# The residual of a decoder's first layer: from load, add and store to accumulating stores onto a copy of x in DRAM

## The chip, the cores and the metric

The kernel runs on one core of one Trainium2 chip. The metric is the device time of one execution in microseconds (us). One further execution was taken with the hardware profiler; its rows are what the text quotes. Engines are named as the profile names them: PE does matmuls, PEld its weight loads, DVE, ACT and POOL work on tiles in on-chip memory, SP only issues transfers. A q behind a name (SPq) is that engine's instruction queue.

## What is computed

Two layers of a decoder over 2048 positions of width 1024. The first layer normalises x, multiplies it with one large input projection, runs four heads of forgetting attention and four of stick-breaking attention, multiplies their outputs with a gate, multiplies with an output projection and adds x. The second layer does the like with three groups of dilated windows.

```python
def even_layer(x, g_norm, w_in, b_f, g_q, g_k, w_out):
    h = rmsnorm(x, g_norm)
    proj = h @ w_in
    ...
    mixed = jnp.concatenate([merge_heads(fox), merge_heads(sb)], axis=-1) * jax.nn.silu(gate)
    return x + mixed @ w_out
```

The change is about the last line: the sum `x + mixed @ w_out`, called x1 here, 2048 x 1024 numbers of four bytes, 8.39 MB. The second layer reads x1 twice: at its start, to normalise it, and at its end, for its own residual.

## The kernel before

**Products.** Every large product is split into panels: 1024 rows of the left side (a round, `r`) by 512 columns. `panel_steps` (L261) computes a panel with seven products of half the size, by the recursive scheme that needs seven where the plain one needs eight, and each number is split into a high and a low part, so that a product is three matmuls (`mm3`, L88, its lines 91 to 93). The names A11, A12, S2, S3, S1, A22, S4 are the seven left and right factors. A panel ends in four results, each of two tiles `c` of 128 x 512 in PSUM plus the parts kept before. `result` (L307) makes each `c` with a DVE addition (L300) in a buffer of the tag `res`, of which there are four, and hands it to an emitter.

**Right factors.** `Weights` (L184) loads quarters of the weight matrix into four buffers `wraw` (L216, SP's queue, 512 KB each). POOL forms the sums and differences among them (L226). ACT writes the high part (L81), DVE or POOL the low part (L86), into one of four buffers `wop`, which PE multiplies with. `get` (L251) keeps three of them ready.

**Left factors.** `left` (L342) reads the transposed input back from DRAM in pieces `lp` (L362), forms sums with DVE and POOL (L345) and splits them (L81 and L86).

**The output projection of the first layer** has four panels: two rounds of rows, two halves of columns. Its emitter is `residual` (L947): for each `c` it loads the 256 x 256 block of x that belongs to it into a tile `x1t` (L953), adds on DVE (L954) and stores the sum into x1 (L955). There are 32 such blocks. Both transfers stand in SP's queue. When a round's x1 is stored, `transpose_to` (L153) loads its rows (L157), normalises and transposes them for the second layer.

**Order.** The program text is emitted by Python generators, and a list scheduler then orders the instructions of each engine by its own model of durations, with the data dependencies as bounds. Each engine takes its queue strictly in order, and an instruction that waits for a semaphore holds up all that stands behind it on its engine. Transfers are issued by SP alone in the kernel before; the launch line (L1334) sets `dynamic_dma_scratch_size=512`, the bytes of a partition that are kept for the descriptors of transfers that POOL issues.

Of the kernel before, what the change touches and what calls it, by code (L numbers as in the profile page):

```python
# [12 lines left out]
OP = mybir.AluOpType  # L13
# [4 lines left out]
P = 128  # L18
# [18 lines left out]
class K:  # L37
# [28 lines left out]
    def c2(self, shape=(P, CH), dt=F32, name="c2", tag="c"):  # L66

        return self.cs.tile(list(shape), dt, name=name, tag=tag, bufs={"c": 4, "res": 4}.get(tag, 2))
# [439 lines left out]
def identity(k):  # L508
    jp = k.c2([P, P], name="jp")
    k.nc.gpsimd.iota(jp, pattern=[[1, P]], base=0, channel_multiplier=-1,  # L510
                     allow_small_or_imprecise_dtypes=True)
    k.ident = k.consts.tile([P, P], F32, name="ident")
    k.nc.vector.tensor_scalar(k.ident, jp, 0.0, None, op0=OP.is_equal)
# [47 lines left out]
def each(emit):  # L561

    def run(block, half, cs):
        for g, c in enumerate(cs):
            emit(block, half, g, c)
    return run
# [188 lines left out]
def merged(*gens):  # L755

    live = [[g, n, 0] for g, n in gens]
    while live:
        live.sort(key=lambda e: (e[2] + 0.5) / e[1])
        e = live[0]  # L760
        if next(e[0], "end") == "end":
            live.remove(e)
        e[2] += 1

def even_attention(k, tail):
    tc, nc = k.tc, k.nc
    c2 = k.c2
    scale = float(P) ** -0.5  # L770
# [2 lines left out]
    def load_head(kind, h):  # L773
        T, V = (k.fT, k.v["f"]) if kind == "f" else (k.sT, k.v["s"])
        kt = k.big([P, 4, 2, CH], F32R, name="kt")
        vt = k.big([P, 4, 2, TPC, P], F32R, name="vt")

        def chunk(c):
            s = slice(c * CH, (c + 1) * CH)
            nc.sync.dma_start(kt[:, c].bitcast(F32), T["k"][:, h, :, s].bitcast(F32))  # L780
            for z in range(2):
                nc.sync.dma_start(vt[:, c, z].bitcast(F32),
                                  V[s, z, h * P:(h + 1) * P].rearrange("(j p) d -> p j d", p=P).bitcast(F32))

        heads[kind, h] = kt, vt
        return chunk

    def load_q(kind, h, u):
        T = k.fT if kind == "f" else k.sT
        if kind == "f" and u % 2 == 0:  # L790
            c = u // 2
            bias[h, c] = c2(name="bias")
            nc.sync.dma_start(bias[h, c], k.ncum[h:h + 1, c * CH:(c + 1) * CH].to_broadcast([P, CH]))
        q = c2([P, 2, 2 * P], F32R, name="qT", tag="q")
        nc.sync.dma_start(q.bitcast(F32), T["q"][:, h, :, u * 2 * P:(u + 1) * 2 * P].bitcast(F32))
        return q
# [52 lines left out]
    def pv(kind, h, u, rows):  # L849

        vt = heads[kind, h][1]
        po = k.ps("s" if kind == "f" else "t")
        gt = c2([P, 2 * P], name="gate", tag="pT")
        m = (0 if kind == "f" else 4) + h
        cols = slice(u * 2 * P, (u + 1) * 2 * P)
        nc.sync.dma_start(gt, k.gT[:, m, cols])

        def transposed(jj):
            pt = k.ps("t")
            hl = k.wps.tile([P, 2, 2, 2 * P], F32R, name="pT", tag="wp")  # L860
            for jx in range(2):
                for i in range(jx if jj == u else 0, 2):
                    nc.tensor.transpose(pt[:, (jx * 2 + i) * P:(jx * 2 + i + 1) * P],  # L863
                                        rows[:, i, (jj * 2 + jx) * P:(jj * 2 + jx + 1) * P], k.ident)
            flat = [hl[:, z].rearrange("p j t -> p (j t)") for z in range(2)]
            for s in (slice(0, 2 * P), slice(3 * P, 4 * P)) if jj == u else (slice(0, 4 * P),):
                k.split(flat[0][:, s], flat[1][:, s], pt[:, s])
            return hl

        ready = transposed(0)  # L870
        for jj in range(u + 1):
            yield
            hl = ready
            if jj < u:
                ready = transposed(jj + 1)
            for jx in range(2):
                j = jj * 2 + jx
                i0 = P if jj == u and jx else 0
                a = [vt[:, j // TPC, z, j % TPC] for z in range(2)]
                k.mm3(po[:, i0:2 * P], a, [hl[:, z, jx, i0:] for z in range(2)], j == 0, j == 2 * u + 1)  # L880
        nc.vector.tensor_tensor(gt, po[:, :2 * P], gt, op=OP.mult)
        nc.sync.dma_start(k.mixT[:, m, cols], gt)
# [3 lines left out]
    def slopes(g, hf):  # L886

        t = k.w4([P, HG, 2, P], name="slopes")
        for h in range(HG):
            slope = 2.0 ** (-8.0 * (g * HEADS + hf * HG + h + 1) / (3 * HEADS))  # L890
            nc.gpsimd.tensor_scalar(t[:, h], k.dist, -slope32(slope) * GROUPS[g][1], 1.0, op0=OP.mult, op1=OP.mult)
        nc.sync.dma_start(k.bias[g, hf], t)
# [10 lines left out]
    for n, (kind, h, u) in enumerate(units):  # L903
        rows = k.big([P, 2, S], name="rows")
        rest = k.big([P, 2, S], name="rest") if kind == "s" else None
        gens = [(qk(kind, h, u, q, rows, rest), 2 * (u // 2 + 1))]
        if n + 1 < len(units):
            q = load_q(*units[n + 1])
        if (kind, h, u) == ("f", 0, 0):
            k.table()  # L910
        nxt = order.index((kind, h)) + 1
        if u == 1 and nxt <= 6:
            slopes((nxt - 1) // 2, (nxt - 1) % 2)
        if nxt < len(order) and u >= 3:
            if u == 3:
                chunk = load_head(*order[nxt])
            else:
                chunk(u - 4)
        if len(past) == 2:
            v = past.pop(0)  # L920
            gens.append((pv(*v[0], v[1]), v[0][2] + 1))
        merged(*gens)
        past.append(((kind, h, u), rows))
        if nxt == len(order) and u in (5, 6):

            tail()
# [4 lines left out]
def odd_layer(k, x, x1, even_w_out, w_in, w_out, out):  # L931
    tc, nc = k.tc, k.nc
    c2, dr = k.c2, k.dram
# [13 lines left out]
    def residual(r, n):  # L947
        def emit(block, half, g, src):
            t0 = r * ROUND + block * CH + g * 256
            c0 = n * CH + half * 256  # L950
            view = lambda d: d[t0:t0 + 256, c0:c0 + 256].rearrange("(r p) c -> p r c", p=P)
            a = c2([P, 2, 256], name="x1t")
            nc.sync.dma_start(a, view(x))  # L953
            nc.vector.tensor_tensor(a, src.rearrange("p (r c) -> p r c", r=2), a, op=OP.add)  # L954
            nc.sync.dma_start(view(x1), a)  # L955
        return each(emit)

    def two(A, emits, tick, after=None):
# [337 lines left out]
@with_exitstack  # L1296
def tile_hybrid_trunk(ctx, tc, x, even_norm, even_w_in, even_b_f, even_q_gain, even_k_gain, even_w_out,
                      odd_norm, odd_w_in, odd_q_gain, odd_k_gain, odd_w_out, out):
    k = K(ctx, tc)
    k.table()  # L1300
    x1 = k.dram.tile([S, D], F32, name="x1d")
    A = []
    spare = []
    first = left_direct(k, x[0], even_norm, A, spare)
    next(first)
    identity(k)
    late = lambda: constants(k, k.cs, even_norm, odd_norm, even_b_f, even_q_gain, even_k_gain, odd_q_gain, odd_k_gain)
    even_projection(k, x[0], even_w_in[0], first, A, spare, late)
    odd = odd_layer(k, x[0], x1, even_w_out[0], odd_w_in[0], odd_w_out[0], out[0])
    W, first = next(odd)  # L1310

    def tail():
        W.ahead(1)
        next(first)

    even_attention(k, tail)
    k.table()
    next(odd, None)

# [27 lines left out]
```

## Time and profile before

| | us |
|---|---|
| median of three runs | 2823.75 |
| lowest and highest of them | 2819.15, 2825.49 |
| the profiled execution, its own time | 2826.53 |
| its span in the trace | 2824.8 |
| first L953 to last L955 in that trace | 1281.3 to 1534.4 |

The span is what the trace covers; the time of the same execution is 1.7 us more. A row of a group of instructions gives the line, the engine, the output and input tiles, shapes and count, then the busy time and the mean of one in nanoseconds, then the idle time of the engine just before these instructions and what ended it. In a list of waits, a row is the waiting instruction, the one waited for, the time in total, how often, and the longest. A row of a stretch gives its length and each engine's busy time with the count of instructions, then the granted clock of PE, the busy share of the 16 DMA engines, and GB/s.

### The profile page before, as it was taken

How to read it: one execution, taken by the hardware profiler on the slowest of the kernel's cores; microseconds unless marked ns; L12 is line 12 of the kernel's file. 1: busy time of each engine (PE TensorE's matmuls, PEld its weight loads, DVE VectorE, ACT ScalarE, POOL GpSimd, SP SyncE). 2: the span in 40 equal slices, each digit the busy share in tenths (PEclk: the TensorE clock that was granted, in tenths of full speed). 3: DMA queues.
4: the chain of work that ended last, by engine and by line, in shares of the span. 5: the costliest groups of instructions: out<-in, count | busy, mean ns of one | idle time of the engine just before them, and what ended most of it. 6: DMA issues, size and time to landing. Idle time of an engine off the chain costs nothing.

```text
span 2824.8 us, 55621 instructions
## 1 busy us (share of the span) xinstructions
PE 2676.4 (95%) x20191; PEld 2455.5 (87%) x20191; DVE 2052.7 (73%) x4373; ACT 1618.6 (57%) x3924; POOL 1223.4 (43%) x981
## 2 busy tenths in 40 slices
PE   6999999999999999998987999999989999999998
PEld 5898878998787789987887999999889999999876
DVE  7857684684888888888959857476797686763966
ACT  6465553454776666665364555555664577665642
POOL 3545464544544433326545544343245432422322
PEclk9999999999999999999998999999999999999999
DMA  5576544445433344435577553334543445444675
GB/s 180 181 222 210 172 160 154 154 142 192 144 111 118 112 123 144 139 104 173 187 232 246 154 179 107 121 122 146 169 128 126 139 140 166 132 147 134 219 254 183
DMA packets 398770, 449.43 MB, mean 159 GB/s; under 512 B 31712, under 2 KB 331040, under 8 KB 398496
## 3 DMA queue, kind: packets, MB, share of 16 engines
q1 hardware_dynamic: 398496, 445.89, 49.4%
q8 instruction: 159, 2.61, 0.4%
q14 instruction: 115, 0.94, 0.1%
HBM read 291.22 MB, written 154.57 MB: 158 GB/s over the span
## 4 chain that ended last, share of the span: by engine, by line
PE 62%; DVE 21%; DMA 7%; ACT 5%; issue 3%; POOL 1%; SPq 1%; DVEq 0%; ACTq 0%; POOLq 0%
PE ps L91 17%; PE ps L93 17%; PE ps L92 17%; DVE rest L828 4%; PE ps L863 2%; PE ps L1145 2%; DVE wop L86 2%; DVE A L86 2%; PE ps L1135 2%; PE ps L1116 2%; DVE lp L345 1%; DVE S L86 1%; PE ps L1061 1%; DVE pT L86 1%; DVE c L300 1%
## 5 line engine op out<-in xcount | busy, mean ns | idle before, releaser
L226 POOL TENSOR_TENSOR wraw<-wraw 128x512 f32<-128x512 f32 (+1 forms) x320 | 444.2, 1400 | 430.3 <-DVE wop L86 157.1
L81 ACT ACTIVATE wop<-wraw 128x512 fp32r<-128x512 f32 (+1 forms) x560 | 349.5, 629 | 383.4 <-PE ps L93 294.2
L86 POOL TENSOR_TENSOR wop<-wraw,wop 128x512 fp32r<-128x512 f32 (+1 forms) x240 | 329.4, 1375 | 534.0 <-ACT wop L81 503.8
L92 PE MATMUL ps<-wop,S 128*128 128x256 f32 (+1 forms) x1792 | 512.4, 286 | 18.1 <-DVE wop L86 16.8
L91 PE MATMUL ps<-wop,A 128*128 128x256 f32 (+1 forms) x1792 | 512.0, 287 | 14.2 <-DVE c L300 13.5
L91 PE MATMUL ps<-wop,S 128*128 128x256 f32 (+1 forms) x1792 | 515.8, 289 | 9.9 <-DVE c L300 6.3
L92 PE MATMUL ps<-wop,A 128*128 128x256 f32 (+1 forms) x1792 | 511.7, 286 | 2.2 <-DVE wop L86 1.5
L93 PE MATMUL ps<-wop,S 128*128 128x256 f32 (+1 forms) x1792 | 512.9, 287 | 0.0
L93 PE MATMUL ps<-wop,A 128*128 128x256 f32 (+1 forms) x1792 | 509.5, 285 | 0.0
L86 DVE TENSOR_TENSOR wop<-wraw,wop 128x512 fp32r<-128x512 f32 (+1 forms) x320 | 270.2, 845 | 232.0 <-ACT wop L81 230.6
L92 PEld LDWEIGHTS ps<-wop,S 128*128 128x128 f32 x1792 | 343.3, 192 | 21.0 <-DVE wop L86 17.8
L91 PEld LDWEIGHTS ps<-wop,A 128*128 128x128 f32 x1792 | 342.3, 191 | 19.0 <-issue 13.4
L91 PEld LDWEIGHTS ps<-wop,S 128*128 128x128 f32 x1792 | 342.1, 191 | 15.1 <-issue 8.4
L92 PEld LDWEIGHTS ps<-wop,A 128*128 128x128 f32 x1792 | 342.9, 191 | 4.0 <-DVE wop L86 3.2
L93 PEld LDWEIGHTS ps<-wop,S 128*128 128x128 f32 x1792 | 342.7, 191 | 3.3 <-issue 2.6
L93 PEld LDWEIGHTS ps<-wop,A 128*128 128x128 f32 x1792 | 342.7, 191 | 1.4 <-issue 0.8
L300 DVE TENSOR_TENSOR c<-u,ps 128x512 f32<-128x512 f32 (+1 forms) x274 | 178.7, 659 | 91.9 <-PE ps L93 86.1
L81 ACT ACTIVATE pT<-ps 128x512 fp32r<-128x512 f32 (+2 forms) x352 | 165.5, 504 | 135.6 <-PE ps L863 81.3
L831 POOL TENSOR_TENSOR rows<-rows,rest 128x512 f32<-128x512 f32 (+4 forms) x160 | 152.6, 957 | 162.1 <-DVE rest L828 141.8
L86 DVE TENSOR_TENSOR pT<-ps,pT 128x512 fp32r<-128x512 f32 (+2 forms) x352 | 188.0, 559 | 44.2 <-ACT pT L81 42.8
L1128 ACT ACTIVATE row<-row,nm 128x256 f32<-128x256 f32 (+1 forms) x384 | 172.5, 452 | 64.4 <-DVE nm L1126 63.9
L92 PE MATMUL ps<-pT,vt 128*128 128x256 f32 x576 | 171.1, 299 | 5.5 <-DVE pT L86 5.3
(214 smaller groups left out, 6485.0 us busy)
## 6 DMA issues: line engine op xcount, KB each, us to landing
wraw<-in_odd_w_in_dram SPq DMA_DIRECT2D x88, 512.0 KB, 4.0
wraw<-in_even_w_in_dram SPq DMA_DIRECT2D x70, 512.0 KB, 4.2
ld<-qk SPq DMA_DIRECT2D x106, 256.0 KB, 3.2
qk<-c SPq DMA_DIRECT2D x96, 256.0 KB, 2.4
lp<-hT SPq DMA_DIRECT2D x60, 256.0 KB, 3.6
uu<-ot SPq DMA_DIRECT2D x96, 132.0 KB, 1.9
fin<-uu SPq DMA_DIRECT2D x16, 792.0 KB, 4.5
hT<-te SPq DMA_DIRECT2D x48, 256.0 KB, 4.3
```

The costliest lines, as they stand in the source:

```text
L81: nc.scalar.activation(hi, src, AF.Copy)
L86: (nc.vector if lo_on == "dve" else nc.gpsimd).tensor_tensor(lo, src, hi.bitcast(F32), op=OP.subtract)
L91: mm(out, a[0], b[0], start=start, stop=False, skip_group_check=more)
L92: mm(out, a[0], b[1], start=False, stop=False, skip_group_check=more)
L93: mm(out, a[1], b[0], start=False, stop=stop, skip_group_check=more)
L226: tt = lambda e, o, x, y, op, s: e.tensor_tensor(o[:, s], x[:, s], y[:, s], op=op)
L300: nc.vector.tensor_tensor(out[g], x[g], y[g], op=OP.add)
L828: nc.vector.tensor_tensor_scan(o[:, b:b + n][:, ::-1], back, k.ident[:, :1].to_broadcast([P, n]), 1.0 if carry is None else carry, OP.mult ...
L831: nc.gpsimd.tensor_tensor(dst[:, :w], dst[:, :w], o[:, b + 1:b + 1 + w], op=OP.mult)
L863: nc.tensor.transpose(pt[:, (jx * 2 + i) * P:(jx * 2 + i + 1) * P], rows[:, i, (jj * 2 + jx) * P:(jj * 2 + jx + 1) * P], k.ident)
L1116: nc.tensor.matmul(scores(hp, e), q[pr, za, hp], ring[pr, zb, hp, blocks], start=i == 0, stop=i == 2)
L1128: nc.scalar.activation(row[:, h // 2, h % 2, :nk], row[:, h // 2, h % 2, :nk], AF.Exp, bias=nm[:, h:h + 1], accum_out=ot[:, HW + HG + h:HW ...
```

## The change

DVE's addition and the tile `x1t` go. For each 128 rows x 256 columns of `c`, POOL now issues a transfer that adds onto what stands in x1 (`accum_op=OP.add`): 64 of 128 KB in place of 32 loads and 32 stores of 256 KB. So that x1 holds x by then, SP copies x to x1 in DRAM in 16 transfers of 512 KB. The calls of the copies are put among the units of the first layer's attention, but nothing in their data binds them to that place.

```diff
-def even_attention(k, tail):
+def even_attention(k, tail, residual):
...
         nxt = order.index((kind, h)) + 1
+        if n % 4 == 1:
+            residual(n // 4)
         if u == 1 and nxt <= 6:
...
             view = lambda d: d[t0:t0 + 256, c0:c0 + 256].rearrange("(r p) c -> p r c", p=P)
-            a = c2([P, 2, 256], name="x1t")
-            nc.sync.dma_start(a, view(x))
-            nc.vector.tensor_tensor(a, src.rearrange("p (r c) -> p r c", r=2), a, op=OP.add)
-            nc.sync.dma_start(view(x1), a)
+            for i in range(2):
+                nc.gpsimd.dma_start(view(x1)[:, i], src[:, i * 256:(i + 1) * 256], accum_op=OP.add)
         return each(emit)
...
-    even_attention(k, tail)
+    def residual(i):
+        k.nc.sync.dma_start(x1[i * P:(i + 1) * P], x[0][i * P:(i + 1) * P])
+
+    even_attention(k, tail, residual)
```

The launch line is unchanged and becomes L1337. Where the scheduler puts the new transfers is seen in the order of the instructions. On POOL, in the output projection of the first round of rows (the rows L226, L345 and L86 are the right factors' sums, the left factors' sums and the low parts), there stood before:

```order
L226 TENSOR_TENSOR wraw<-wraw 128x512 x2
L86 TENSOR_TENSOR wop<-wraw,wop 128x2x256
L226 TENSOR_TENSOR wraw<-wraw 128x512 x2
L86 TENSOR_TENSOR wop<-wraw,wop 128x2x256 x3
L345 TENSOR_TENSOR lp<-lp 128x512
L226 TENSOR_TENSOR wraw<-wraw 128x512 x7
```

and now, in the same projection (L955 is the accumulating transfer):

```order
L955 DMA x1d<-c 128x256 x4
L226 TENSOR_TENSOR wraw<-wraw 128x512 x2
L955 DMA x1d<-c 128x256 x4
L226 TENSOR_TENSOR wraw<-wraw 128x512 x2
L955 DMA x1d<-c 128x256 x4
L226 TENSOR_TENSOR wraw<-wraw 128x512 x2
L86 TENSOR_TENSOR wop<-wraw,wop 128x2x256 x2
L226 TENSOR_TENSOR wraw<-wraw 128x512 x2
L86 TENSOR_TENSOR wop<-wraw,wop 128x2x256
L345 TENSOR_TENSOR lp<-lp 128x512
L86 TENSOR_TENSOR wop<-wraw,wop 128x2x256
L955 DMA x1d<-c 128x256 x8
```

The 64 transfers stand in 20 groups of two to eight, between the sums and splits that feed PE; 44 of them directly follow another.

On SP, at the start of the program, behind the load of the last small constant (`ok`), there stood before:

```order
L546 DMA ok<-in_odd_k_gain_dram 128x64
L216 DMA wraw<-in_even_w_in_dram 128x4x256 x3
L673 DMA sqT<-fb 128x512 x3
L216 DMA wraw<-in_even_w_in_dram 128x4x256
L673 DMA sqT<-fb 128x512
```

and now:

```order
L546 DMA ok<-in_odd_k_gain_dram 128x64
L1317 DMA x1d<-in_x_dram 16x8192 x6
L216 DMA wraw<-in_even_w_in_dram 128x4x256
L1317 DMA x1d<-in_x_dram 16x8192 x2
L216 DMA wraw<-in_even_w_in_dram 128x4x256
L1317 DMA x1d<-in_x_dram 16x8192 x8
L216 DMA wraw<-in_even_w_in_dram 128x4x256
L673 DMA sqT<-fb 128x512 x3
```

All 16 copies (L1317) have moved ahead of the whole first layer, among the first weight loads. On DVE, in the same projection as above, there stood before (x1t is the tile of the residual):

```order
L300 TENSOR_TENSOR c_15852<-u3_15671,ps_15794 128x512 [waits DVE_49,PE_49]
L345 TENSOR_TENSOR stage_15650<-stage_15650,lp_16084 128x512 [waits DVE_49]
L954 TENSOR_TENSOR x1t_15856<-c_15852,x1t_15856 128x512 [waits DMAHW2_49,DVE_49]
L300 TENSOR_TENSOR c_15853<-u3_15671,ps_15795 128x512 [waits PE_49]
L86 TENSOR_TENSOR wop_15895<-wraw_15471,wop_15895 128x2x256 [waits Activation_49]
```

The additions that make `c` (L300) now wait for POOL's transfers (DMASW is the semaphore of one of these), because a buffer of `c` is free only when its two transfers have landed:

```order
L300 TENSOR_TENSOR c_15860<-u3_15679,ps_15802 128x512 [waits DMASW0_49,DMASW1_49,DVE_49,PE_49]
L300 TENSOR_TENSOR c_15861<-u3_15679,ps_15803 128x512 [waits DMASW2_49,DMASW3_49,DVE_49,PE_49]
L86 TENSOR_TENSOR wop_15899<-wraw_15483,wop_15899 128x2x256 [waits Activation_49]
L300 TENSOR_TENSOR c_15926<-u3_15679,ps_15868 128x512 [waits DMASW5_49,DMASW4_49,PE_49]
L345 TENSOR_TENSOR lp_16301<-lp_16301,lp_16303 128x512 [waits DMAHW3_49,DMAHW4_49,DMAHW0_49,Pool_49]
L300 TENSOR_TENSOR c_15927<-u3_15679,ps_15869 128x512 [waits DMASW7_49,DMASW6_49,PE_49]
```

L954 is gone there, and the waits for DMASW have come to L300.

## Prediction

> **What bounds the kernel now.** I read the page first, then stretches, then the output projection by itself.
>
> ```profile
> span 2824.8 us, 55621 instructions
> PE 2676.4 (95%) x20191; PEld 2455.5 (87%) x20191; DVE 2052.7 (73%) x4373; ACT 1618.6 (57%) x3924; POOL 1223.4 (43%) x981
> ```
>
> PE is busy for 95% of the span, so time can be won only where PE waits. The view of stretches (busy time and count of PE, PEld, DVE, ACT, POOL, then clock, DMA share, GB/s) shows such a place:
>
> ```profile
> 1320.00:1535.00 215.00, 177.92 (x1394) 174.47 (x1394) 173.14 (x234) 107.10 (x234) 119.72 (x77) 0.92 0.71 232
> 1535.00:1750.00 215.00, 202.12 (x1689) 198.42 (x1687) 155.38 (x303) 116.03 (x297) 119.83 (x87) 0.96 0.48 152
> ```
>
> The first stretch holds 31 of the 32 old additions. PE idles there for 215 - 178 = 37 us, in the equal stretch behind it for 13 us. DVE is the busiest of the others (173 us), POOL has 215 - 120 = 95 us idle, and the DMA engines are at 71%. PE's longest waits in this stretch, and the chain that ended last in it by line, say who is late:
>
> ```profile
> PE ps L92 <- DVE wop L86: 13.7, 6, 8.4
> PE ps L91 <- DVE c L300: 11.5, 2, 10.3
> ...
> by line: issue 13.0%; DVE S L86 9.6%; DVE x1t L954 7.1%; DVE A L86 6.4%; DVE wop L86 5.7%; DMA hT<-te 5.3%; DVE c L300 4.5%; PE ps L91 3.7%; DVE lp L345 3.7%; ACT te L149 3.6%; PE ps L92 3.5%; PE ps L93 3.4%; DMA x1t<-in_x_dram 3.2%; DMA lp
> ```
>
> PE waits for DVE, and DVE's queue holds the additions of the residual.
>
> **What goes.** 32 additions, of which 31 lie in the stretch:
>
> ```profile
> L954 DVE TENSOR_TENSOR x1t<-c,x1t 128x512 f32<-128x512 f32 x31 | 31.2, 1008 | 9.0 <-DMA x1t<-in_x_dram 8.9
> ```
>
> DVE loses 31.2 us of work and 9.0 us of waiting. On the chain it was 7.1% + 3.2% of 215 us = 22 us (the additions, and the loads of x that they waited for). That is the most that the removal can give; what is late next is DVE's splitting of S and A, which stays. SP loses 64 issues at about 0.37 us each, which nobody waited for by themselves. The 8.39 MB of loads of x leave the stretch; an accumulation has to read the same bytes of x1 again, so the DMA engines are not relieved.
>
> **What is added on POOL.** 64 transfers. POOL issues none in the trace of before, so the cost is bounded by the nearest rows: SP's issue of the old store, and its time from issue to landing.
>
> ```profile
> L955 SPq DMA_DIRECT2D x1d<-x1t x32: 359/370/1312, 1320.0 to 1534.4; - x32
> ...
> DMA to landing us min/median/max: 2.1/4.1/8.4
> ...
> mixT<-gate SPq DMA_DIRECT2D x64, 128.0 KB, 2.1
> ```
>
> From below it is 0.37 us, if POOL only hands the transfer over. From above it is the whole time to landing, if POOL cannot write the next one's descriptors until the last one is through. Between the two stands POOL's own kind of work, 1.5 to 1.6 us an instruction:
>
> ```profile
> L226 POOL TENSOR_TENSOR wraw<-wraw 128x512 f32<-128x512 f32 x32 | 47.7, 1514 | 11.1 <-DMA wraw<-in_even_w_out_dram 9.8 <-DVE wop L86 1.3
> L86 POOL TENSOR_TENSOR wop<-wraw,wop 128x512 fp32r<-128x512 f32 x24 | 38.3, 1599 | 42.6 <-ACT wop L81 26.9 <-ACT lg L106 15.7
> ```
>
> I take the upper bound. The reason is in the program: L1337 keeps 512 bytes of a partition for the descriptors of POOL's transfers. A transfer here has 128 rows, each of which is read in two places (`c` and x1) and written in one, over 16 DMA engines; I judge that so small a store holds one such transfer and not two, so that a transfer directly behind another waits until that one has landed. [...] No run so far shows it.
>
> For the landing I take 4.1 us, the median of the old stores of 256 KB, since an accumulation of 128 KB carries as much: 128 KB out of `c` and 128 KB read from x1. Its lower end is 2.1 us, which is also what a plain 128 KB store takes, its upper end 8.4 us. So:
>
> - 44 transfers directly behind another: 44 x 4.1 = 180 us.
> - 20 behind one to fifteen other POOL instructions of some 1.5 us, half of the landing hidden: 20 x 2.05 = 41 us.
> - POOL's own work in the stretch: 119.7 us, of which nothing goes.
>
> The sum is 341 us in a stretch of 215 us: POOL becomes the bound, and +126 us is left over. None of it can hide. Behind the waiting transfers stand L226 and L86, which make the right factors for PE, with three `wop` kept ready, some few us of PE's work; and DVE's L300 waits for the landing of the transfers four tiles back, with DVE's L86 behind it in its queue. POOL still has to wait for ACT and for weights at times; of its 95 us idle I add 10 us. The removed 22 us are then worth nothing, since they were DVE's.
>
> [...]
>
> **What is added at the start.** The 16 copies move 8.39 MB. In the first 25 us the DMA engines moved 274 GB/s at 82% busy:
>
> ```profile
> 0.00:25.00 25.00, 8.78 (x36) 7.47 (x37) 14.63 (x33) 18.03 (x40) 3.33 (x9) 1.00 0.82 274
> 50.00:75.00 25.00, 18.84 (x122) 16.65 (x121) 24.29 (x34) 13.63 (x28) 21.40 (x15) 0.81 0.32 112
> ...
> 23.16 9.60 SPq L216 DMA_DIRECT2D wraw<-in_even_w_in_dram  x3
> 40.30 0.39 SPq L216 DMA_DIRECT2D wraw<-in_even_w_in_dram  x1
> 48.24 0.38 SPq L216 DMA_DIRECT2D wraw<-in_even_w_in_dram  x1
> ...
> 53.11 3.01 POOL L226 TENSOR_TENSOR wraw<-wraw 128x512 f32<-128x512 f32 x2
> ...
> 70.85 0.80 PE L93 MATMUL ps<-A,wop 128*128 128x512 f32 x1 [4.20 <-DVE wop L86]
> ```
>
> At that rate they take 31 us, from 23 us on, and the three weight loads that stood at 23 to 33 us are now interleaved with them, the last behind all 16. The loads at 40 and 48 us follow in the queue, and the first sums that need them begin on POOL at 53.1 us. If all of this slips, the copies cost up to 31 us less the slack; I reckon that the copies end near 23 + 31 = 54 us and the last load comes some 6 us late. DVE, busy for 24.3 of the 25 us, is what PE waits for at 70.85 us, so part of that is covered: +4 us, with 0 and 30 us as ends.
>
> **The sum.** 126 + 10 + 4 = +140 us on the profiled execution's own 2826.5 us (span 2824.8 us and 1.7 us around it) gives 2966 us. The median of the runs lies 2.8 us lower, so I forecast 2963 us, 4.9% slower.
>
> **The rivals.**
>
> *POOL pays for the writing alone* (slower, but little): the store of descriptors holds several transfers, and one costs what POOL's other instructions cost, 1.5 us. 64 x 1.5 = 96 us; with its own 120 us POOL is at 216 of 215 us. For it speaks that POOL sat idle for 95 us; against it that idle time came in pieces before other engines' results (26.9 us before ACT's L81 in the row of L86), so they can't all be filled. I give it +20 us after a few us from DVE: about 2845 us, between 2830 and 2870. Chance 0.14.
>
> *The change does what it is written to do* (faster): a transfer costs POOL 0.37 us as it costs SP, 64 x 0.37 = 24 us, and fits in the 95 us. Then DVE's 22 us on the chain come off, less 4 us at the start: 2824 - 18 = 2806 us. For it speaks that DVE is what PE waits for; it decides as long as a transfer holds POOL for less than about 1 us. Chance 0.10.
>
> *No change*: a transfer holds POOL for about 1 us, and what DVE gains POOL and the start give back: 2818 to 2829 us. Chance 0.04.
>
> My forecast has the remaining 0.72. Its own range has the landing as its largest unknown: at 2.1 us the sum is 92 + 21 + 120 = 233 us, +18 us with 10 for waits, 2852 us; at 6.25 us, halfway between median and longest, 275 + 62 + 120 = 457 us, +242 us and 14 more, 3080 us.
>
> **The range and the chances.** Eight times in ten: 2840 to 3070 us. That leaves out the faster case and no change (0.14) and about 0.06 of the ends. Within 0.2%, or 5.6 us, is about what a measurement of this kernel can't tell from no change: its three runs spread over 6.3 us. Faster by more than that 0.10, within it 0.04, slower 0.14 + 0.72 = 0.86.
>
> **What would show it right or wrong.** Right: in the stretch of the output projection, some 350 us long, POOL has no room, the time between two L955 in a row is near the landing of the first, POOL's rows L226 and L86 stand idle behind L955, and PE's longest waits there are for wop (POOL's or, behind it, DVE's) or for DVE's L300 that waits for a transfer. Wrong: two L955 in a row within 1.5 us of each other while the first is still under way; then the descriptors fit, and one of the rivals holds. Wrong as well if PE's waits at 50 to 75 us grow by tens of us: then the copies are the cost, and not POOL. If the stretch gets shorter than 215 us, DVE's additions were worth what the chain says.

## The result, and the profile after

| | us |
|---|---|
| before, median of four runs beside the changed kernel | 2824.62 |
| after, median of four runs | 2951.48 (2945.13 to 2953.09) |
| ratio, with its 95% interval | 1.0443 (1.0431 to 1.0456) |
| span of the profiled execution, before and after | 2824.8 and 2951.3 |

The change costs 127 us; 140 were forecast. Where they arise is found by following the same instruction through both traces. The last L881, the gates at the end of the first layer's attention, starts at 1312.2 us before and 1318.4 after: +6. The first L1018, behind the output projection, starts at 1547.1 and 1678.4: +131. The last store of the result, L1274, is at 2821.2 and 2947.7: +126.5. So 125 us are lost in the output projection and 6 ahead of it, and about 5 are given back behind it.

The view of stretches of the kernel after (columns as in the prediction) has the projection:

```profile
1324.00:1662.00 338.00, 203.46 (x1412) 197.94 (x1410) 152.99 (x209) 109.99 (x237) 160.54 (x141) 0.77 0.53 128
```

For nearly as many matmuls as before (1412 records, 1394 before) the projection takes 338 us in place of 215. PE idles for 135 us of it, where it idled for 37: of the 123 us by which the stretch has grown, 98 are PE's idle time, and 25 are a longer busy time for the matmuls. DVE is down from 173 to 153 us of work. POOL's share looks modest, 161 of 338 us, because the 138.1 us that it waits ahead of its transfers are not counted as busy. The view of the source line of the transfers shows them:

```profile
L955 POOL DMA_DIRECT2D x1d<-c x64: 862/881/1023, 1324.6 to 1660.8; - x64
...
  issue: 138.1, 44
...
DMA to landing us min/median/max: 3.1/3.1/7.8
```

"issue" is idle time for which the profile sees no other instruction as the cause. It comes 44 times, 138.1 us in all or 3.14 us each. With POOL's 160.5 us of work that is 299 of 338 us. 41 of the 44 stand ahead of a transfer that directly follows another. The other three such transfers wait as well, 8.7 us in all, but there the profile names an instruction of ACT or DVE as the cause; and three waits called "issue" stand ahead of the first transfer of a group. On the chain that ended last in this stretch, "issue" of all engines together is 37.9% of 338 us, or 128 us, where it was 13.0% of 215 us, or 28 us, before. One group in the timeline of POOL (start, duration, and in brackets the idle time ahead and its cause) shows the wait:

```profile
1524.15 0.89 POOL L955 DMA_DIRECT2D x1d<-c  x1 [2.62 <-issue]
1530.31 0.87 POOL L955 DMA_DIRECT2D x1d<-c  x1 [5.26 <-issue]
1533.73 0.88 POOL L955 DMA_DIRECT2D x1d<-c  x1 [2.55 <-issue]
```

In each cycle 0.88 us is POOL's own record of the transfer (its writing, as it is called here; no row shows what POOL does in it), and the rest is waiting. The view of L955 narrowed to one transfer at a time gives the landing of each, counted from its own start. The first of these three lands after 5.8 us, and the second starts 6.16 us behind it; the second lands after 3.1 us, and the third starts 3.42 us behind it. So it is for all 44 transfers that directly follow another: the transfer ahead takes between 3.1 and 6.0 us to land, 3.7 on average, and the next one starts 0.26 to 0.36 us after that landing. The longest waits of PE in the same stretch, ACT's wait for POOL and DVE's for a transfer say who passes it on:

```profile
PE ps L92 <- POOL wop L86: 57.1, 7, 15.5
PE ps L91 <- ACT wop L81: 50.5, 6, 16.8
...
ACT wop L81 <- POOL wraw L226: 89.8, 11, 26.8
...
DVE c L300 <- DMA x1d<-c: 9.9, 2, 5.7
```

Before, PE waited 1.4 us for POOL's L86 there. Now it waits 57 us for it and 50 us for ACT's L81, which in turn waits 90 us for what POOL's L226 has to sum (29.5 us before). L86 and L226 are the instructions that stand in POOL's queue behind the transfers. DVE's own wait for a landing, 9.9 us in two places, is small.

At the start, the copies and the loads beside them keep the DMA engines busy for the whole of a 25 us stretch, and the sums that stood at 53.1 us begin at 62.5 us:

```profile
25.00:50.00 25.00, 23.54 (x114) 19.06 (x114) 21.75 (x34) 13.88 (x29) 5.17 (x4) 1.00 1.00 351
...
62.53 10.40 POOL L226 TENSOR_TENSOR wraw<-wraw 128x512 f32<-128x512 f32 x6 [5.93 <-DMA wraw<-in_even_w_in_dram]
```

Of these 9.4 us three are left at the first L828 (714.7 us before, 717.6 after).

### The profile page after: what moved, and what is told of

Same layout as the page of the kernel before. It is cut to its first block, busy times and chain, and to the rows that moved or that the text cites. A ratio compares the mean times of both kernels' runs of the same rounds, so it can differ in the third digit from the quotient of the medians.

```text
span 2951.3 us, 55618 instructions
## 1 busy us (share of the span) xinstructions
PE 2704.6 (92%) x20191; PEld 2479.0 (84%) x20191; DVE 2025.4 (69%) x4341; ACT 1619.4 (55%) x3924; POOL 1260.5 (43%) x1045
## 3 DMA queue, kind: packets, MB, share of 16 engines
q0 software_dynamic: 9216, 8.39, 2.3%
HBM read 291.22 MB, written 162.96 MB: 154 GB/s over the span
## 4 chain that ended last, share of the span: by engine, by line
PE 60%; DVE 18%; issue 7%; ACT 5%; DMA 4%; POOL 4%; SPq 0%; DVEq 0%; POOLq 0%; ACTq 0%
PE ps L91 16%; PE ps L92 16%; PE ps L93 16%; DVE rest L828 4%; PE ps L863 2%; PE ps L1145 2%; PE ps L1116 2%; PE ps L1135 2%; DVE wop L86 2%; DVE A L86 1%; POOL wraw L226 1%; PE ps L1061 1%; DVE lp L345 1%; DVE pT L86 1%; POOL x1d L955 1%
## 5 line engine op out<-in xcount | busy, mean ns | idle before, releaser
L226 POOL TENSOR_TENSOR wraw<-wraw 128x512 f32<-128x512 f32 (+1 forms) x320 | 445.3, 1414 | 429.7 <-DVE wop L86 156.7
L81 ACT ACTIVATE wop<-wraw 128x512 fp32r<-128x512 f32 (+1 forms) x560 | 349.5, 629 | 460.1 <-PE ps L93 304.5
L91 PE MATMUL ps<-wop,S 128*128 128x256 f32 (+1 forms) x1792 | 520.7, 292 | 65.4 <-ACT wop L81 50.5
L92 PE MATMUL ps<-wop,A 128*128 128x256 f32 (+1 forms) x1792 | 514.7, 287 | 43.2 <-POOL wop L86 43.1
L92 PE MATMUL ps<-wop,S 128*128 128x256 f32 (+1 forms) x1792 | 519.0, 290 | 25.8 <-POOL wop L86 18.9
L86 POOL TENSOR_TENSOR wop<-wraw,wop 128x512 fp32r<-128x512 f32 (+1 forms) x240 | 325.0, 1367 | 492.9 <-ACT wop L81 479.6
L93 PE MATMUL ps<-wop,S 128*128 128x256 f32 (+1 forms) x1792 | 517.6, 289 | 0.0
L86 DVE TENSOR_TENSOR wop<-wraw,wop 128x512 fp32r<-128x512 f32 (+1 forms) x320 | 272.8, 854 | 271.0 <-ACT wop L81 267.9
L91 PEld LDWEIGHTS ps<-wop,S 128*128 128x128 f32 x1792 | 346.6, 194 | 72.3 <-ACT wop L81 54.2
L92 PEld LDWEIGHTS ps<-wop,A 128*128 128x128 f32 x1792 | 345.2, 193 | 45.3 <-POOL wop L86 44.1
L92 PEld LDWEIGHTS ps<-wop,S 128*128 128x128 f32 x1792 | 348.7, 195 | 29.7 <-POOL wop L86 19.5
L93 PEld LDWEIGHTS ps<-wop,S 128*128 128x128 f32 x1792 | 348.6, 195 | 3.2 <-issue 2.6
L300 DVE TENSOR_TENSOR c<-u,ps 128x512 f32<-128x512 f32 (+1 forms) x274 | 178.9, 659 | 146.4 <-PE ps L93 129.7
L81 ACT ACTIVATE pT<-ps 128x512 fp32r<-128x512 f32 (+2 forms) x352 | 165.4, 502 | 138.7 <-PE ps L863 83.2
L86 DVE TENSOR_TENSOR pT<-ps,pT 128x512 fp32r<-128x512 f32 (+2 forms) x352 | 188.0, 559 | 45.4 <-ACT pT L81 43.8
L300 DVE TENSOR_TENSOR u<-u,ps 128x512 f32<-128x512 f32 (+1 forms) x168 | 109.5, 658 | 104.9 <-PE ps L93 104.3
```

What stands on the lines that cost most here:

```text
L81: nc.scalar.activation(hi, src, AF.Copy)
L86: (nc.vector if lo_on == "dve" else nc.gpsimd).tensor_tensor(lo, src, hi.bitcast(F32), op=OP.subtract)
L91: mm(out, a[0], b[0], start=start, stop=False, skip_group_check=more)
L92: mm(out, a[0], b[1], start=False, stop=False, skip_group_check=more)
L93: mm(out, a[1], b[0], start=False, stop=stop, skip_group_check=more)
L226: tt = lambda e, o, x, y, op, s: e.tensor_tensor(o[:, s], x[:, s], y[:, s], op=op)
```

## Theories and experiments

The theory is that of the prediction: the store of descriptors, 512 bytes, holds one accumulating transfer, and POOL stands still until that one has landed. It is theory A here, beside the expectations' theory B. By it two such transfers fit in 576 bytes and three in 960, and three plain ones, or three of 64 rows, in 512; these counts were the author's estimate, and no run had shown them. The main rivals: the writing itself costs POOL's time; an accumulating transfer is slow work for the DMA engines; the copies are in the way. Ratios are to the kernel before, measured beside each kernel, with 95% intervals. Where two kernels have the same order of instructions on every engine, the text says so; where it doesn't, the scheduler has also moved other instructions.

**The size of the store.** Only the launch line is edited, and the order stays that of the changed kernel.

```diff
-dynamic_dma_scratch_size=512
+dynamic_dma_scratch_size=576
```

> The changed kernel with 576 bytes of a partition for POOL's descriptors in place of 512; every engine's instructions are in the same order. [...] Then a second transfer of a group starts right behind the first, and only the third and later odd ones wait: 12 waits of 1.7 to 3.4 us, 20 to 40 us in place of 138 us in 44 waits, and the time falls from 2951 to 2835 to 2865 us. Theory B, transfers that POOL issues, or accumulating ones, follow each other one by one whatever the store is: 44 waits, 138 us, 2951 us.

Measured: 2871.69 us, 1.0165 (1.0148 to 1.0182), 80 us less than with 512 and 7 us above the range that theory A gave. The 28.5 us of waits lie within what was expected, but in 22 pieces and not in 12:

```profile
L955 POOL DMA_DIRECT2D x1d<-c x64: 862/888/1552, 1325.5 to 1577.0; - x64
...
  issue: 28.5, 22
```

With 960 bytes:

```diff
-dynamic_dma_scratch_size=512
+dynamic_dma_scratch_size=960
```

> The changed kernel with 960 bytes for POOL's descriptors, which is what the on-chip memory still has room for; the same order. [...] Here the two rivals of the prediction part: if what DVE lost was worth 22 us, 2806 to 2815 us; if POOL's 57 us of writing are too much for its pieces of idle time, 2830 to 2850 us. Theory B: 2951 us, as with 512 bytes.

Theory A put the waits under 15 us and the time between 2810 and 2845 us. Measured: 2852.17 us, 1.0093 (1.0078 to 1.0108): 7 us above that range and 2 us above that of the rival by which POOL's writing is too much for its idle time. Line, one group of four, and stretch:

```profile
L955 POOL DMA_DIRECT2D x1d<-c x64: 832/1048/1921, 1320.4 to 1551.2; - x64
...
  issue: 18.0, 15
...
DMA to landing us min/median/max: 3.1/4.9/8.1
...
1372.01 2.68 POOL L955 DMA_DIRECT2D x1d<-c  x3
```

```profile
1324.00:1564.00 240.00, 189.25 (x1418) 185.62 (x1418) 163.89 (x209) 108.11 (x234) 163.04 (x142) 0.86 0.75 186
```

64 bytes more take away 110 us of waiting on POOL and 80 us of time, and nothing else was touched. So the room in the store is the cause of at least 99 of the 127 us; with 960 bytes 15 waits are still there.

How many transfers fit is seen in the rows of POOL. With 512 bytes each transfer in a row waits for the one ahead. With 960 bytes the group above has three without a pause, in 2.68 us, and the fourth waits 1.6 us. In the 20 groups 44 transfers stand behind the first, 24 behind the second and 15 behind the third; "issue" comes 44, 22 and 15 times.

So one, two and three accumulating transfers are under way with 512, 576 and 960 bytes; for 576 this is read from the number of waits. If each takes the same room, that is more than 256 and at most 288 bytes, an estimate from one in 512 and two in 576; what the room is made of is not shown.

Each transfer also lands later when several are under way: the median is 4.9 us with 960 bytes, 4.1 us with 576 and 3.1 us with 512.

**Plain transfers.** The same order again, without the addition; the residual is left out.

```diff
-nc.gpsimd.dma_start(..., accum_op=OP.add)
+nc.gpsimd.dma_start(...)
```

> The changed kernel with 512 bytes, but POOL's 64 transfers overwrite x1 in place of adding to it (the residual is left out of x1, so the output is not the reference's); the same order and the same waits on semaphores. [...] Theory B in the form that any two transfers of POOL follow one by one: 138 us of waits and 2951 us. Theory B in the form that only accumulating ones do: this run falls, and the run with 960 bytes does not.

Theory A put the waits under 20 us and the time between 2815 and 2850 us. Measured: 2833.47 us, 1.0036 (1.0023 to 1.0050), with 13.2 us of waits.

```profile
L955 POOL DMA_DIRECT2D x1d<-c x64: 539/548/736, 1316.6 to 1529.8; - x64
...
  issue: 13.2, 11
```

The same number of transfers through the same 512 bytes costs little, since more than one plain transfer fits: the group at 1366.9 us has three without a pause, and the fourth waits 2.64 us. Each also takes POOL 0.55 us in place of 0.88. So neither POOL's transfers as such nor the 512 bytes alone make POOL wait for each landing, but the two together with the accumulation. With 960 bytes (the launch line edited as above):

> Plain transfers (nothing is added, the residual is left out) with 960 bytes for descriptors in place of 512; the order of the instructions is that of the changed kernel. With 512 bytes it took 2833 us and POOL's transfers waited 13.2 us for nothing that the profile shows (11 times). Theory (waiting for room in the descriptor store is what is left to gain here): the waits fall below 3 us and the time to 2820-2829 us. Rival (those waits lay beside other waits of POOL and cost nothing; what is left is POOL's writing, 35 us, and the copies): the waits fall as well, the time stays at 2830-2838 us.

Measured: 2835.57 us, 1.0026 (1.0012 to 1.0040). The waits are gone, and the time has not fallen: the rival holds. The 13 us of waits, in pieces, cost nothing that can be seen. POOL now waits 27.1 us for DVE's `c` there, where it waited 15.5 us with 512 bytes:

```profile
  DVE c L300: 27.1, 10
...
  issue: 0.3, 1
```

**What the removal is worth.** The kernel before, with DVE's addition and the loads of x left out (so the residual is missing): SP stores `c` as it is.

```diff
-            nc.sync.dma_start(a, view(x))
-            nc.vector.tensor_tensor(a, src..., a, op=OP.add)
-            nc.sync.dma_start(view(x1), a)
+            nc.sync.dma_start(view(x1), src...)
```

> The kernel before, with c stored to x1 by SP as it is: no load of x, no addition on DVE, no transfer of POOL, no copies (the residual is left out, so the output is not the reference's). It bounds what the removal alone can give. Theory of the prediction: 22 us, the share of the chain, so 2803 us (2798 to 2808). Rival, raised by the run with plain stores, which was 8 us slower than before although DVE had lost its 31 us: the additions were on the chain, but what stood behind them was as late, and the removal is worth under 8 us: 2817 to 2826 us.

Measured: 2805.81 us, 0.9926 (0.9909 to 0.9942), 21 us less than before. The stretch is 17 us shorter, and PE idles in it for 24 us where it idled for 37:

```profile
1320.00:1518.00 198.00, 173.84 (x1381) 171.13 (x1380) 139.75 (x203) 104.70 (x230) 111.92 (x77) 0.94 0.68 215
```

**The copies.** The kernel before, with the 16 copies of x to a tensor that nobody reads:

```diff
+        if n % 4 == 1:
+            residual(n // 4)
...
+    x2 = k.dram.tile([S, D], F32, name="x2d")
+    def residual(i):
+        k.nc.sync.dma_start(x2[i * P:(i + 1) * P], x[0][i * P:(i + 1) * P])
```

> The kernel before with the 16 copies of x added, to a place that nothing reads; they stand at the start, as in the changed kernel. Theory: they cost the 3 us (2 to 6) by which the first scan came later: 2827 to 2831 us. Rival: what they delay is caught up later, as with the copies held back, where the time stayed the same: 2822 to 2827 us. If the copies were the main cost at the start, up to 30 us: 2840 to 2855 us.

Measured: 2831.53 us, 1.0021 (1.0011 to 1.0031), +4.7 us. And the changed kernel with the copies bound to their place in the program, so that they go out one by one during attention:

```diff
-        k.nc.sync.dma_start(x1[i * P:(i + 1) * P], x[0][i * P:(i + 1) * P])
+        k.tc.keep_in_program_order(k.nc.sync.dma_start(x1[i * P:(i + 1) * P], x[0][i * P:(i + 1) * P]))
```

> The changed kernel with 512 bytes, its 16 copies held behind what stands before them in the program text on SP, so that they go out one by one in the first layer's attention and not at the start. Theory: the copies at the start cost the 2.9 us by which the first scan of the stick-breaking attention (L828) came later (717.6 against 714.7 us), and nothing where they stand now: 2946 to 2950 us, L828 starting at 714 to 715 us. Rival 1: all of the 6 us lost before the output projection came from the copies: 2943 to 2946 us. Rival 2: the copies cost the same wherever they stand: 2951 us.

Measured: 2952.12 us, 1.0451 (1.0433 to 1.0468): no gain, as the second rival said. In one trace of each, the first L828 stands at 715.7 us in place of 717.6, the last L881 at 1314.0 in place of 1318.4, but the first L1018 at 1676.9 in place of 1678.4. Of the 4 us that are won ahead of the projection, 1.5 are left at its end.

**Half and half.** 960 bytes, one of each two blocks accumulated, the other loaded, added and stored as before:

```diff
+            if g:
+                a = c2([P, 2, 256], name="x1t")
+                nc.sync.dma_start(a, view(x))
+                nc.vector.tensor_tensor(a, src..., a, op=OP.add)
+                nc.sync.dma_start(view(x1), a)
+                return
             for i in range(2):
                 nc.gpsimd.dma_start(..., accum_op=OP.add)
```

> 960 bytes, and only one of the two tiles c of each result is added by POOL's accumulating transfers, the other by DVE as before; the copies stay. 32 accumulating transfers take 29 us of POOL and 34 us of the 16 DMA engines, half of what the run with 960 bytes had. Theory: POOL's writing and the DMA engines' time are what is left of the cost, so half of the 27 us goes: 2833 to 2843 us. Rival: with room on POOL, DVE's relief shows: 2812 to 2822 us.

Measured: 2846.27 us, 1.0068 (1.0047 to 1.0090), slightly above what was expected. Waits for room are gone from POOL's rows, and POOL's writing is halved (26.8 us for 30 of its 32 transfers in place of 61.4 for 64 with 960 bytes). But DVE is busy for 195 of 236 us, more than the 173 of 215 before, though half of its additions are gone; its splits `wop` (L86) take 48.4 us (33 of them) in place of 28.0 (32). Why they take longer is not shown, and the order of the instructions is another one here.

**Smaller transfers.** The changed kernel with each transfer cut into two of 64 rows, 128 in all. This edit also made the scheduler rearrange every engine.

```diff
-    nc.gpsimd.dma_start(view(x1)[:, i], src[:, ...], accum_op=OP.add)
+    for e in range(2):
+        q = slice(e * 64, (e + 1) * 64)
+        nc.gpsimd.dma_start(view(x1)[q, i], src[q, ...], accum_op=OP.add)
```

> The changed kernel with 512 bytes, each accumulating transfer split in two of 64 rows. [...] Theory B, any transfer of POOL waits for the one in front of it: 108 waits of at least 2.5 us, 270 us, more than 3050 us.

Theory A put the waits at 48 to 80 us and the time between 2880 and 2910 us. Measured: 2935.39 us, 1.0381 (1.0362 to 1.0401), a miss by 25 us.

```profile
L957 POOL DMA_DIRECT2D x1d<-c x128: 812/922/2025, 1324.4 to 1639.6; - x128
...
  issue: 54.8, 48
```

The waits did fall, from 138 to 55 us. But a transfer of half the size takes POOL about as long to write (0.81 us at least, against 0.86), and there are twice as many: most of what was gained in waiting was paid again in writing (112 us in place of 56.5). The same kernel with 960 bytes (the launch line edited as above; same order as with 512):

> Accumulating transfers of 64 rows, 128 of them, with 960 bytes for descriptors; the order of the instructions is that of the 64-row kernel with 512 bytes (2935 us, waits of 54.8 us), which is not that of the changed kernel. In both theories the waits shrink below 25 us. Theory (with room enough, what the accumulation still costs is POOL's time for writing descriptors): 64 instructions more at about 0.87 us are 56 us more of POOL's time in the stretch than the 128-row kernel with 960 bytes has (2852 us), some of it beside POOL's idle time: 2870-2905 us. Rival (what it still costs is the transfers' own work on the DMA engines, which the splitting leaves as it is): within 8 us of the 128-row kernel, 2844-2860 us.

Measured: 2912.21 us, 1.0293 (1.0276 to 1.0311). Waits for room are 3.7 us there, and the time is 60 us above that of the 128-row transfers with 960 bytes. That is what the theory of writing said, but the other order of instructions stands between the two. So a last pair with one order, the 64-row transfers with 960 bytes, plain (`accum_op` is left out, and with it the residual):

> Plain transfers of 64 rows, 128 of them, with 960 bytes for descriptors (nothing is added, the residual is left out). The order of the instructions is that of the accumulating 64-row kernel with 960 bytes (2912 us, 122 us of writing on POOL, waits of 3.7 us). The writing should be near 128 x 0.5 = 64 us, as much as the accumulating 128-row kernel's 61 us, with a third of its packets. Theory (what the accumulation costs beyond room in the store is POOL's writing, at about one us of time for one us of writing): 2912 less 122 - 64 = 58 us, so 2840-2865 us. Rival (it is the transfers' own work on the DMA engines, three times that of plain ones): only the 17 us that lay between accumulating and plain transfers of 128 rows with 960 bytes come off, 2885-2900 us.

Measured: 2880.27 us, 1.0186 (1.0169 to 1.0203), 32 us less than accumulating: between the two expectations, so it settles nothing between them. Writing is 66.7 us there (128 at a median of 0.521 us).

It is also 45 us slower than the plain 128-row transfers, for 32 us more of writing and another order of instructions. How much of the 45 us, and of the 60 us above, is the order's and how much the writing's is not shown.

## Why the prediction was right, point by point

**The account.** The kernels give each part a price:

| part | pair of kernels | us |
|---|---|---|
| DVE's additions and the loads of x go | before, then stores of `c` by SP | -21 |
| 16 copies of x | before, then with copies | +5 |
| what is left over: 64 plain stores on POOL for 32 on SP, and another order | 2806 + 5 = 2811, then plain, 960 bytes | +25 |
| the transfers accumulate | plain, then accumulating, 960 bytes (one order) | +17 |
| room for one transfer in place of three | 960 bytes, then 512 (one order) | +99 |

The last two rows are measured directly, each between kernels of one order. The +25 us are only what remains when the first two rows are added up, so that the sum, +125 us, comes near the measured +127 by its making and is no check. The kernel before itself took 2824.6 to 2827.5 us beside these runs, and differences of 3 us say nothing.

**POOL waits until the one ahead has landed: right.** Each of the 44 transfers that were said to wait starts about 0.3 us after the landing of the one ahead, and the store's size alone moves the waits called "issue" from 138.1 to 28.5 and 18.0 us. The price was good too: 44 x 4.1 = 180 us were put down, and a follower's whole cycle is 0.88 us of writing and 3.15 us of waiting, 4.03 us or 177 us for all. The 4.1 us were the median of another engine's stores of twice the bytes, and that they came so near is partly luck: the median landing here is 3.1 us, and only the average, 3.7 us, with 0.3 us behind it gives 4.0.

**20 group-starters at 2.05 us: too much.** They were to wait for half a landing. 17 of them pay their 0.88 us of writing and no "issue": what POOL does between two groups is mostly as long as a landing. Three, with one or two sums or splits between, wait 8.3 us. Together that is 26 us and not 41.

**Other waits of POOL, +10 us: too small, and POOL's own work too large.** POOL's own rows in the stretch add up to 118 us, about as taken. But the next instruction on POOL begins about 0.57 us after a transfer has begun, so 14 us of these rows run beside the writing, and only 160.5 - 56.5 = 104 us are added to the stretch where 119.7 were taken. What is left of the 338 us, 31, are waits for DVE, ACT and weights, where 10 were taken. The errors are -3, -15, -16 and +21 us: they cancel to -13, the difference between the 351 us that the sum implied and the measured 338. That the forecast came so near is in this part luck. The low end of the range, 2852 us, leaves out the 4 us of the start that the high end has; nothing hangs on it.

**How PE is starved: right in one half.** PE waits for `wop`, which POOL's L86 and, by way of ACT, POOL's L226 deliver late. That ACT's L81 would hand on half of it was not said. The second path, DVE's L300 held by a landing and DVE's L86 behind it, hardly matters: 9.9 us of waits for a landing, and PE's waits for DVE's `wop` in the row of L92 fell from 13.7 to 6.0 us.

**DVE's 22 us: right in both halves.** They were read from the chain as the most the removal could give, and 21 us came off when nothing took their place. That they are worth nothing in the changed kernel, where POOL is late, fits the rows, but no run tries it.

**The start, +4 us: right in size.** The copies by themselves cost 4.7 us; the changed kernel is 6 us late at the last L881. The first sums slipped by 9.4 us and not by 6, of which a third is left at the first L828. In the changed kernel the 4 us were not a term of their own, though: with the copies held back the time stayed where it was.

**The rivals.** *POOL pays for the writing alone* was forecast at 2845 us, and this is near what comes once there is room: 2852 us, with 61 us of writing where 96 were assumed. Whether the 27 us above the kernel before are the writing's is not shown, since 15 waits and later landings remain beside it. *The change does what it is written to do* had as its condition that a transfer holds POOL for less than about 1 us. Written without a wait it holds it for 0.83 us or more, and even the plain one, 0.54 us, ended above the kernel before. That condition was too generous. The likely reason is the one that the prediction held against the other rival: POOL's 95 idle us in the old stretch came in pieces before other engines' results.

**What stays open.** What the 17 us of accumulating over plain transfers are made of, with 960 bytes: 26 us more of writing on POOL, 15 waits for room, or the work of the DMA engines. POOL's queue has three times as many packets and three times the time for the same 8.39 MB: 9216 packets and 28.5% of 16 engines' 240 us when accumulating (68 us), 3072 and 10.7% of 216 us when plain (23 us). The pair of 64-row kernels could not separate them. And no version that adds the residual came out ahead of the kernel before. What remains to be won is at most the 21 us of the removal, of which the copies take 5 and the change to plain stores on POOL, with its order, 25.

## What to carry to other kernels

Moving the store from SP to POOL turned an issue of 0.37 us on SP, which nothing waited for, into 0.55 us (plain) or 0.88 us (accumulating) of POOL's queue, and with 512 bytes kept for descriptors an accumulating store that directly followed another waited for that one's landing as well (44 of them); look for idle time called "issue" ahead of each transfer that directly follows another, and try more room before anything else, since 64 bytes were worth 80 us here. Price a moved instruction on the engine that receives it by what stands behind it in that queue, not by the engine's mean idle time. When an edit makes a scheduler rearrange the program, compare only kernels of one order, or take the order itself for a suspect.

## What the runs showed of the hardware that was not expected

- An accumulating transfer of 128 KB, 128 rows of 1 KB, is 144 packets where a plain one is 48 (9216 and 3072 for 64). Over the stretch from 1320 to 1553 us, with 960 bytes, the accumulating ones took 29.0% of 16 engines' time for 8.26 MB, 122 GB/s; a plain kernel's took 10.7% of 216 us for 8.39 MB, 363 GB/s. For the same bytes the accumulating ones keep the DMA engines busy three times as long; the prediction had taken the second read for twice the work. No row counts a second read: POOL's queue has 8.39 MB with the addition and without it, and the page's HBM reads are 291.22 MB before and after, with the copies' reads of x in the place of the old loads.
- Writing an accumulating transfer takes POOL 0.88 us, a plain one 0.55 us; halving the rows hardly shortens either (0.81 and 0.52 us at the least).
- PE's matmuls themselves were slower in the starved stretch: 203.46 us for 1412 in place of 177.92 for 1394, or 144 and 128 ns each, at a granted clock of 0.77 in place of 0.92. Over these kernels the clock is lower where PE idles more: 0.94, 0.92, 0.86 and 0.77 at 24, 37, 51 and 135 us of idle time (before without the addition, before, 960 bytes, 512 bytes). The order is not strict: with 576 bytes it is 0.88 at 67 us. What sets the clock is not shown. The 25 us of longer busy time in the stretch are what the lower clock can have cost there; no run separates it.
